# Output products of block 0 ahead of block 1's, its residual and norm among them, and three weight splits in fixed places

## The chip, the cores and the metric

The kernel runs on one core of a Trainium2 chip. The core has five engines with an instruction queue each: TensorE (PE, the matrix products), VectorE (DVE), ScalarE (ACT), GpSimd (POOL) and SyncE (SP, which here issues the weight DMAs). Each engine takes its instructions in order and waits on semaphores for the others. The metric is the device time of one execution in microseconds (us).

## The reference

A two-layer transformer trunk on 256 tokens of width 1024, in f32. Cut to what matters:

```python
def mixer_ab(h, ...):                # layer 0: two groups of attention heads
    ...
    return jnp.concatenate([ya, yb], axis=-1) @ w_out      # 1024 x 1024, "wo"

def squared_relu_mlp(h, w1, w2):
    return jnp.square(jax.nn.relu(h @ w1)) @ w2            # 1024 -> 4096 -> 1024
# every layer, twice (mixer, then MLP):
#   h = x * (1 + scale) + shift                            # "mod", from the conditioning c
#   x = LN(alpha * x + gate * sublayer(h))
```

The scales, shifts and gates ("ada") are products of the conditioning vector with large weights that are read as the kernel runs.

## The kernel before

**Tiles.** The 256 tokens are two blocks, b = 0 and 1, of 128 partitions. Products are done in f32r with both operands split into a high and a low part: `wh`, `wl` for weights, `yTh`, `yTl` for the attention's output transposed, `hTh`, `hTl` for the modulated activations. Each product is three matmuls into one accumulator (`mm3`, L236 to L238). A split is one cast on ACT (L170) and one subtraction on DVE (L171; on POOL for "wo").

**The weight stream.** `plan` is the list of all weight tiles (1 MB each) in the order in which they are used. SP issues their DMAs (L164) into four raw buffers; `take` splits the next tile in two halves into buffers of a pool of six (`wh`) and six (`wl`), so a split waits until earlier products have read the buffer. `need(key)` takes tiles until `key` is there. Tiles of the first MLP are ("w1", 0, i) and ("w2", 0, i); a half is named with a last number, ("w1", 0, 1, 0). The "ada" tiles stand among them.

**Order.** The kernel is written as one program, from which a scheduler makes each engine's order by priority: what was written earlier goes first, among what it expects to be ready. `later(n)` moves what stands in it n places back in priority (negative: ahead); `LATER` is the table of such numbers by step or half tile. A dependency without semaphore (`behind`, used elsewhere in the kernel) only fixes the order of two instructions on one engine.

**The stage around the change.** `mixed_out` runs the output projection of layer 0's mixer. It is driven by strings of steps. The first two run beside the attention of the two blocks ("under"), the third after it:

- Ybj: half j of block b's attention output is transposed (PE, L585), copied and split to yT (ACT L482, L170; DVE L171).
- Obhk: output product of block b, half h of the 1024 columns, half k of the 1024 inputs: 12 matmuls of 128x512 into `ps_out`. O with (h, k) reads weight tile wo_(2h+k). There are two accumulator buffers: (0,0) and (1,0) take them first, then (0,1), (1,1).
- G: the gate row, broadcast.
- Rbh: residual of half h (`residual`): product with the gate (DVE L610, frees the accumulator), plus alpha x (L611), statistics (L612).
- Nb: `norm`: aggregate of the statistics (DVE L616), add epsilon to `rs` (L618), power -1/2 on POOL (L302), then normalise z in two halves (DVE L627).
- Mb: `modulate`: eight PE transposes of z to `ps_mod` (L444), scale and shift to h (ACT L449, for block 1's second half DVE L452), split to hT (L170, L171).

Block 1's M1 and the new x are issued from the MLP: `first_tokens(i, b)` are the first two tiles of the MLP's first product for one block, 24 matmuls of 128x256 into `ps_m` each; `second(i, b, h)` the second product; `first(i)` both blocks at once.

`renew` does R, N, M after the MLP in the same manner, and layer 1's mixer ends in another `mixed_out`, whose strings already have `N0` among block 1's products.

Of the kernel before, what the change touches and what calls it, by code (L numbers as in the profile page):

```python
# [22 lines left out]
ALU = mybir.AluOpType  # L23
# [7 lines left out]
LN_EPS = 1e-5  # L31
# [11 lines left out]
NSPLIT = 6  # L43

SPLITS_LATER, ADA_LATER, ROWS_LATER = 200, 300, 0
LATER = {("ci", 0, 0): -1000, ("ci", 0, 1): -1000, ("co", 1, 1): -300, ("wo", 2, 0): 400, ("ada", 1, 5): 500, "cM1": 30, "cO011": -300, "cO100": 100, "wO000": 60, "wO100": 60, "wO001": 60, "wO010": 60, "wO011": 60, "wO110": -40, "wY10": -80}

X_STEPS = ({8: 4, 9: 4}, 13), ({i: 1 for i in range(3, 11)}, 12)

# [15 lines left out]
def trunk(ctx: ExitStack, tc, c, x, pos, small, ln, ada, w_g, w_g1, w_uq, w_out, c_in, c_out, w1, w2, out):  # L65
    nc = tc.nc
# [19 lines left out]
    def col(shape, name, bufs=4, dtype=F32):  # L86
        return work.tile(shape, dtype, name=name, tag=name, bufs=bufs)


    def by_tensor(key):  # L90

        return key[0] == "ada" and (key[1] == 0 and key[2] >= 8 or key[1] == 1 and key[2] < 6)

    @contextmanager
    def later(n):

        if not n:
            yield
            return
        at = tc.cur_priority  # L100
        tc.cur_priority = at + n
        yield
        tc.cur_priority = at + (tc.cur_priority - at - n)
# [34 lines left out]
    raw, parts, state = {}, {}, {"next": 0, "taken": 0, "half": 0, "critical": None, "rows": None, "copied": None, "columns": None}  # L138
# [5 lines left out]
    def fill():  # L144
        while state["next"] < len(plan) and state["next"] < state["taken"] + NRAW + direct():
            key = plan[state["next"]]
            src = source[key[0]](*key[1:])
            if key[0] in ("g", "g1"):
                cuts, tag = ((0, 712, 1424), "wl") if key[0] == "g" else ((0, 1024), "wh")
                parts[key] = []  # L150
                for lo, hi in zip(cuts, cuts[1:]):
                    t = sp.tile([P, 1024], F32, name="w_" + key[0], tag=tag)[:, :hi - lo]
                    nc.sync.dma_start(t, src[:, lo:hi])
                    parts[key].append(t)
                state["next"] += 1
                if key == ("g1", 0):
                    load_early(1)
                continue
            t = wp.tile([P, 2048], F32, name="w_" + "_".join(map(str, key)), tag="w")
            if key[:2] == ("ada", 0) and key[2] < 8:  # L160
                for j in range(2):
                    nc.sync.dma_start(t[:, j * D:(j + 1) * D], src[:, j * D:(j + 1) * D])
            else:
                nc.sync.dma_start(t[:, :src.shape[1]], src)  # L164
            raw[key] = t
            state["next"] += 1

    def split(dh, dl, src, eng=nc.vector):

        nc.scalar.copy(dh, src)  # L170
        return eng.tensor_sub(dl, src, dh.bitcast(F32))  # L171

    def take():

        key = plan[state["taken"]]
        w = raw.get(key)
        if w is None:
            pass
        elif key[0] == "uq":
            parts[key] = [w[:, :1024], w[:, 1024:]]  # L180
        elif by_tensor(key):
            with later(ROWS_LATER):
                ada_rows(key, w)
        elif key[0] == "ada":
            j = state["half"]
            with later(LATER.get(key, ADA_LATER)):
                state["half"] = ada_product(key, j, w[:, j * D:(j + 1) * D])
            if state["half"]:
                return
        else:  # L190
            cuts = (0, 1024, 2048)
            parts[key] = []
            for part, (lo, hi) in enumerate(zip(cuts, cuts[1:])):
                if key in (("w1", 0, 0), ("w1", 1, 0), ("w2", 0, 15)):
                    wh, wl = (work.tile([P, 1024], F32R, name=n, tag="q4", bufs=5) for n in ("wh", "wl"))
                elif key in (("wo", 0), ("co", 0)):
                    if lo == 0:
                        wide = [t.rearrange("p k q -> p (k q)") for t in new_hT()]
                    wh, wl = wide[0][:, lo:hi], wide[1][:, lo:hi]
                else:  # L200
                    wh = sp.tile([P, 1024], F32R, name="wh", tag="wh")[:, :hi - lo]
                    wl = sp.tile([P, 1024], F32R, name="wl", tag="wl")[:, :hi - lo]
                half = (*key, part)
                with later(LATER.get(half, SPLITS_LATER)):
                    split(wh, wl, w[:, lo:hi], nc.gpsimd if key[0] == "wo" else nc.vector)
                parts[key].append((wh, wl))
        state["taken"] += 1
        fill()
# [10 lines left out]
    def need(key):  # L219
        while place[key] >= state["taken"]:  # L220
            take()
        if by_tensor(key):
            ada_columns()
            ada_end()
        return parts.get(key)
# [75 lines left out]
    def rsqrt(dst, src):  # L301
        state["pow"] = nc.gpsimd.tensor_tensor(out=dst, in0=src, in1=mhalf, op=ALU.pow)  # L302
# [15 lines left out]
    def ada_product(key, j, w):  # L318

        junk = work.tile([P, D], BF16, name="junk", tag="junk", bufs=1)  # L320
        m, bias = ada_bias(key, j)
        state[key, j] = nc.vector.tensor_tensor_reduce(out=junk, in0=w, in1=cB, scale=1.0, scalar=bias,  # L322
                                                       op0=ALU.mult, op1=ALU.add, accum_out=m)
        if j == 1:
            ada_factors(key)
        return 1 - j

    def behind(what, m):

        if what in state:  # L330
            tc.add_manual_dep(m.ins, state[what].ins.name, mybir.DependencyInfo(
                mybir.DependencyClass.NoSync, mybir.DependencyReason.DATA))
# [6 lines left out]
    def ada_rows(key, w):  # L339

        ada_columns()
        ps = pa("ps_ada")
        for k in range(KT):
            g = slice(32 * (k % 4), 32 * (k % 4 + 1))
            in_turn(nc.tensor.matmul(ps[g, :256], cT[:, k:k + 1].to_broadcast([P, 32]),
                                     w[:, 256 * k:256 * (k + 1)], start=k < 4, stop=k >= 4))
        state["rows"] = key, ps
# [85 lines left out]
    def new_hT():  # L435
        return [hp.tile([P, KT, 256], F32R, name=n, tag=n) for n in ("hTh", "hTl")]
# [152 lines left out]
    def new_yT(b):  # L589
        hi = work.tile([P, KT, P], F32R, name="yTh", tag="q4", bufs=5)  # L590
        if b == 0:
            return hi, work.tile([P, KT, P], F32R, name="yTl", tag="q4", bufs=5)
        lo = work.tile([P, 1040], F32R, name="yTl", tag="vv", bufs=2)[:, :D]
        return hi, lo.rearrange("p (n q) -> p n q", n=KT)
# [19 lines left out]
    def moments(st):  # L614
        mv = col([P, 2], "mv")
        nc.vector.bn_aggr(mv, st.rearrange("p a s -> p (a s)"))  # L616
        rs = col([P, 1], "rs")
        nc.vector.tensor_scalar_add(rs, mv[:, 1:2], LN_EPS)  # L618
        rsqrt(rs, rs)
        return mv, rs  # L620

    def norm(b, zst):
        z, st = zst
        mv, rs = moments(st)
        for h in range(2):
            s = slice(h * 512, (h + 1) * 512)
            nc.vector.tensor_scalar(z[:, s], z[:, s], mv[:, 0:1], rs, op0=ALU.subtract, op1=ALU.mult)  # L627

    def new_x(zs, gb):

# [103 lines left out]
    for b in range(NB):  # L734
# [4 lines left out]
                                       op0=ALU.mult, op1=ALU.add, accum_out=ss)  # L739
# [121 lines left out]
    def steps(*todo):  # L861
        for f, *args in todo:
            with later(LATER.get(names[f] + str(args[0]), 0)):
                f(*args)
# [30 lines left out]
    def mixed_out(ys, name, i, first, second, under_first, under_second, after):  # L895
# [7 lines left out]
        def step(s):  # L903
            op, *n = s
            b = int(n[0]) if n else 0
            if op in todo:
                with later(LATER.get(s, 0)):
                    todo[op](b)
            if op == "Y":
                if n[1] == "0":  # L910
                    yT[b] = new_yT(b)
                with later(LATER.get(name[0] + s, 0)):
                    y_half(ys[b], yT[b], int(n[1]))
                if n[1] == "1":
                    zs[b] = new_z()
            elif op == "O":
# [3 lines left out]
                need((name, 2 * h + kq))  # L920
                with later(LATER.get(name[0] + s, 0)):
                    out_part(accs[b, h], yT[b], (name, 2 * h + kq), kq, kq == 0, kq == 1)
# [27 lines left out]
        def rest():  # L950
# [4 lines left out]

    hT, rest = mixed_out(ys, "wo", 0, side(st[4]), side(st[5]),
# [3 lines left out]


    def mlp(l, hT, rest, rows):
# [154 lines left out]
    mv, rs = moments(zs[1][1])  # L1117
    beside_vector(0, slice(672, D), *first, after=state["pow"])
    for s in halves:
        z = zs[1][0]  # L1120
        nc.vector.scalar_tensor_tensor(z[:, s], in0=z[:, s], scalar=mv[:, 0:1], in1=gb[0][:, s],  # L1121
                                       op0=ALU.subtract, op1=ALU.mult)
# [55 lines left out]
```

## Time and profile before

| | us |
|---|---|
| median of 3 runs | 669.85 (668.53 to 671.62) |
| the profiled execution | 669.5 |
| its span in the profile | 667.7 |
| outside the span | 1.8 |
| mean granted PE clock | 0.979 |
| PE busy | 633.5 (95%) |
| DVE busy | 472.7 (71%) |
| ACT busy | 339.8 (51%) |
| POOL busy | 53.6 (8%) |
| DMA, mean over the span | 227 GB/s |

Times in rows of the timeline count from the span's start. The output projection runs until 143, the first MLP from 152 to 341, the MLP's norm and modulation until 351. The name of a tile stands with the line that wrote it: `z<-ps_out,gateB` of L610 is the start of a residual, `wl<-w_w,wh` of L171 a weight split, `z<-z,mv,rs` of L627 a norm. A bracket at a row's end tells how long the engine idled before it and which instruction released it. The granted clock is a share of PE's full clock.

### The profile page before, as it was taken

What the parts mean: (1) busy time and instruction counts of PE and PEld (TensorE: products, weight loads), DVE (VectorE), ACT (ScalarE), POOL (GpSimd) and SP (SyncE); (2) the same over time, 40 slices, a digit from 0 to 9 for tenths busy, and PEclk for the clock granted to TensorE, in tenths of its full rate; (3) what the DMA queues carried; (4) which work ended last, traced back from release to release, by engine and by line L of the source; (5) the groups of instructions that cost most, each with busy time, mean ns of one, the idle gap of its engine ahead of it and who ended that gap; (6) DMA issues with size and microseconds to landing.
All of it is one profiled execution on the core that took longest, in us unless ns stands there. A gap on an engine that the chain in (4) does not pass through costs nothing. (4 is left out here: it accounts for less than half of the span.)

```text
span 667.7 us, 9765 instructions
## 1 busy us (share of the span) xinstructions
PE 633.5 (95%) x3762; PEld 532.3 (80%) x3762; DVE 472.7 (71%) x856; ACT 339.8 (51%) x538; POOL 53.6 (8%) x77
## 2 busy tenths in 40 slices
PE   6998989968999999999989999999999999999994
PEld 3555777857989898988867888888899989898983
DVE  2859998485588889887796996755867755554447
ACT  3324757345554545455544555873654555545440
POOL 5010246100020000100010000000000000000004
PEclk9999998997999999999989999999999999999997
DMA  8993796353588897899843486311467855565101
GB/s 313 407 414 123 264 359 256 126 190 126 189 315 300 322 380 270 330 352 367 311 151 115 171 353 223 140 60 63 151 228 257 310 189 189 200 237 193 66 0 63
DMA packets 24384, 151.50 MB, mean 227 GB/s; under 512 B 2833, under 2 KB 3089, under 8 KB 8338
## 3 DMA queue, kind: packets, MB, share of 16 engines
q1 hardware_dynamic: 24194, 150.71, 61.6%
q8 instruction: 29, 0.48, 0.3%
q10 hardware_dynamic: 144, 0.18, 0.1%
q14 instruction: 17, 0.14, 0.1%
HBM read 149.83 MB, written 1.05 MB: 226 GB/s over the span
## 5 line engine op out<-in xcount | busy, mean ns | idle before, releaser
L171 DVE TENSOR_TENSOR wl<-w_w,wh 128x1024 fp32r<-128x1024 f32 x128 | 153.5, 1221 | 81.3 <-ACT wh L170 81.2
L170 ACT CAST wh<-w_w 128x1024 fp32r<-128x1024 f32 x128 | 131.0, 1050 | 151.6 <-PE ps_m L237 71.0
L236 PE MATMUL ps_m<-hTh,wh 128*128 128x256 f32 x448 | 126.7, 283 | 0.0
L238 PE MATMUL ps_m<-hTh,wl 128*128 128x256 f32 x448 | 126.6, 283 | 0.0
L237 PE MATMUL ps_m<-hTl,wh 128*128 128x256 f32 x448 | 126.6, 283 | 0.0
L322 DVE CUSTOM_DVE_ANT_0 junk<-w_ada,cB,sm 128x1024 bf16<-128x1024 f32 x72 | 95.7, 1328 | 11.1 <-DMA w_ada<-in_ada_dram 9.8
L236 PE MATMUL ps_m<-wh,uh 128*128 128x512 f32 x256 | 101.6, 397 | 0.0
L237 PE MATMUL ps_m<-wl,uh 128*128 128x512 f32 x256 | 101.1, 395 | 0.0
L238 PE MATMUL ps_m<-wh,ul 128*128 128x512 f32 x256 | 101.0, 396 | 0.0
L237 PEld LDWEIGHTS ps_m<-hTl,wh 128*128 128x128 f32 x448 | 85.6, 191 | 1.3
L236 PEld LDWEIGHTS ps_m<-hTh,wh 128*128 128x128 f32 x448 | 85.6, 191 | 1.2
L238 PEld LDWEIGHTS ps_m<-hTh,wl 128*128 128x128 f32 x448 | 85.7, 191 | 0.0
L238 PEld LDWEIGHTS ps_m<-wh,ul 128*128 128x128 f32 x256 | 48.2, 188 | 11.3 <-DVE ul L171 0.2
L236 PEld LDWEIGHTS ps_m<-wh,uh 128*128 128x128 f32 x256 | 48.3, 189 | 10.1 <-ACT uh L170 0.3
L237 PEld LDWEIGHTS ps_m<-wl,uh 128*128 128x128 f32 x256 | 48.2, 188 | 9.7
L236 PE MATMUL ps_c<-wh,hTh 128*128 128x512 f32 x96 | 38.6, 406 | 2.4 <-ACT hTh L170 2.0
L541 ACT ACTIVATE prob<-prob,negm 128x128 f32<-128x128 f32 (+1 forms) x64 | 26.9, 451 | 23.4 <-DVE negm L537 23.4
L171 DVE TENSOR_TENSOR ul<-relu,uh 128x512 fp32r<-128x512 f32 (+1 forms) x36 | 22.7, 630 | 22.7 <-ACT uh L170 22.7
L237 PE MATMUL ps_c<-wl,hTh 128*128 128x512 f32 x96 | 38.8, 405 | 0.0
L238 PE MATMUL ps_c<-wh,hTl 128*128 128x512 f32 x96 | 38.3, 400 | 0.0
L171 DVE TENSOR_TENSOR wl<-w_ci,wh 128x1024 fp32r<-128x1024 f32 x24 | 28.7, 1218 | 5.4 <-ACT wh L170 5.2
L302 POOL TENSOR_TENSOR rs<-rs,mhalf 128x1 f32<-128x1 f32 x8 | 6.6, 824 | 320.5 <-DVE rs L618 320.5
(231 smaller groups left out, 1025.9 us busy)
## 6 DMA issues: line engine op xcount, KB each, us to landing
w_w<-in_w_dram SPq DMA_DIRECT2D x64, 1024.0 KB, 5.1
w_ada<-in_ada_dram SPq DMA_DIRECT2D x40, 1024.0 KB, 6.6
w_ci<-in_c_in_dram SPq DMA_DIRECT2D x12, 1024.0 KB, 5.7
w_ada<-in_ada_dram SPq DMA_DIRECT2D x12, 512.0 KB, 9.5
w_wo<-in_w_out_dram SPq DMA_DIRECT2D x4, 1024.0 KB, 6.1
w_co<-in_c_out_dram SPq DMA_DIRECT2D x4, 1024.0 KB, 5.4
w_g<-in_w_g_dram SPq DMA_DIRECT2D x8, 356.0 KB, 9.1
early<-in_ada_dram SPq DMA_DIRECT2D x4, 512.0 KB, 8.0
```

The costliest lines, as they stand in the source:

```text
L170: nc.scalar.copy(dh, src)
L171: return eng.tensor_sub(dl, src, dh.bitcast(F32))
L236: nc.tensor.matmul(ps, a[0], b[0], start=start, stop=False)
L237: nc.tensor.matmul(ps, a[0], b[1], start=False, stop=False)
L238: nc.tensor.matmul(ps, a[1], b[0], start=False, stop=stop)
L302: state["pow"] = nc.gpsimd.tensor_tensor(out=dst, in0=src, in1=mhalf, op=ALU.pow)
L322: state[key, j] = nc.vector.tensor_tensor_reduce(out=junk, in0=w, in1=cB, scale=1.0, scalar=bias, op0=ALU.mult, op1=ALU.add, accum_out=m)
L541: state["exp"] = nc.scalar.activation(pr[:, j, :nk], pr[:, j, :nk], AF.Exp, bias=negm[:, hd:hd + 1], scale=-1.0)
```

## The change

It does five things:

1. The third string of `mixed_out` begins with O010 and O011, followed by R01, N0 and Y11; O101, O110 and O111 of block 1 follow, with M0 ahead of O101. Before, O010 and O011 stood in the second string, Y11 and O101 came right after R01, and N0 stood with the last product.
2. `BEHIND` ties three half splits on DVE: the first half of w1 tile 1 behind the `rs` of block 0's norm ("moments0"), its second half and the first half of w2 tile 0 behind block 0's norm ("norm0").
3. In `LATER`, steps O001, O010 and O011 lose their 60, O100 goes from 60 to 120 and O101 gets 60.
4. The ada tile (1, 5) loses its 500 and has the usual 300, (1, 6) and (1, 7) get 600.
5. `moments` and `norm` note their instructions for `BEHIND`; this emits nothing.

```diff
-LATER = {... ("wo", 2, 0): 400, ("ada", 1, 5): 500, "cM1": 30, "cO011": -300, "cO100": 100, "wO000": 60, "wO100": 60, "wO001": 60, "wO010": 60, "wO011": 60, "wO110": -40, "wY10": -80}
+LATER = {... ("wo", 2, 0): 400, ("ada", 1, 6): 600, ("ada", 1, 7): 600, "cM1": 30, "cO011": -300, "cO100": 100, "wO000": 60, "wO100": 120, "wO101": 60, "wO110": -40, "wY10": -80}
+
+BEHIND = {("w1", 0, 1, 0): "moments0", ("w1", 0, 1, 1): "norm0", ("w2", 0, 0, 0): "norm0"}
...
                 with later(LATER.get(half, SPLITS_LATER)):
-                    split(wh, wl, w[:, lo:hi], nc.gpsimd if key[0] == "wo" else nc.vector)
+                    behind(BEHIND.get(half), split(wh, wl, w[:, lo:hi], nc.gpsimd if key[0] == "wo" else nc.vector))
...
-        nc.vector.tensor_scalar_add(rs, mv[:, 1:2], LN_EPS)
+        state["moments"] = nc.vector.tensor_scalar_add(rs, mv[:, 1:2], LN_EPS)
...
         mv, rs = moments(st)
+        state["moments%d" % b] = state["moments"]
...
-            nc.vector.tensor_scalar(z[:, s], z[:, s], mv[:, 0:1], rs, op0=ALU.subtract, op1=ALU.mult)
+            state["norm%d" % b] = nc.vector.tensor_scalar(z[:, s], z[:, s], mv[:, 0:1], rs, op0=ALU.subtract, op1=ALU.mult)
...
                          "s1 Y00 | s1 | s1 O000 Y10 | O100",
-                         "G | | Y01 O001 R00 | O010 O011 | R01",
-                         "Y11 O101 | O110 R10 | | O111 N0 | R11 | M0 | N1")
+                         "G | | Y01 O001 R00",
+                         "O010 O011 R01 N0 Y11 | M0 O101 | O110 R10 | O111 R11 | N1")
```

What `behind` does with it:

```python
    def behind(what, m):
        if what in state:
            tc.add_manual_dep(m.ins, state[what].ins.name, ...NoSync...)
```

The order that results is shown at three places. In the names of weight tiles the last number tells them apart: 1037 is w1 tile 0, 1162 w1 tile 1, 1211 w2 tile 0, 1288 w1 tile 2. Lines of the changed kernel are two or three higher.

DVE from the start of R01 (the first multiply) to block 0's norm, before:

```order
L610 TENSOR_TENSOR z<-ps_out,gateB 128x512
L171 TENSOR_TENSOR wl<-w_w_0_0_1037,wh 128x1024
L611 SCALAR_TENSOR_TENSOR z<-x_79,z 128x512
L610 TENSOR_TENSOR z<-ps_out,gateB 128x512
L612 BN_STATS stats<-z 128x6
L611 SCALAR_TENSOR_TENSOR z<-x_81,z 128x512
L616 BN_AGGR mv<-stats 128x2
L171 TENSOR_TENSOR wl<-w_w_0_2_1288,wh 128x1024
L618 TENSOR_SCALAR rs<-mv 128x1
L612 BN_STATS stats<-z 128x6
L627 TENSOR_SCALAR z<-z,mv,rs 128x512 x2
```

And of the changed kernel:

```order
L612 TENSOR_TENSOR z<-ps_out,gateB 128x512
L613 SCALAR_TENSOR_TENSOR z<-x_79,z 128x512
L173 TENSOR_TENSOR wl<-w_w_0_0_1037,wh 128x1024
L614 BN_STATS stats<-z 128x6
L173 TENSOR_TENSOR yTl<-evac,yTh 128x512
L618 BN_AGGR mv<-stats 128x2
L620 TENSOR_SCALAR rs<-mv 128x1
L173 TENSOR_TENSOR wl<-w_w_0_1_1162,wh 128x1024
L630 TENSOR_SCALAR z<-z,mv,rs 128x512 x2
L173 TENSOR_TENSOR wl<-w_w_0_1_1162,wh 128x1024
L173 TENSOR_TENSOR wl<-w_w_0_0_1211,wh 128x1024
```

Block 1's residual (x_81) has left the chain and follows later; the two splits of w1 tile 1, which before came ahead of R01, now stand between rs and the norm and behind the norm.

PE at the end of the output products, before:

```order
L236 MATMUL ps_out<-wh,yTh 128x512
L237 MATMUL ps_out<-wl,yTh 128x512
L238 MATMUL ps_out<-wh,yTl 128x512
L444 MATMUL ps_mod<-ident,z 128x128 x8
L236 MATMUL ps_m_1457<-wh,hTh 128x256
L237 MATMUL ps_m_1457<-wl,hTh 128x256
```

And of the changed kernel, from the tenth product of O111:

```order
L238 MATMUL ps_out<-wh,yTh 128x512
L446 MATMUL ps_mod<-ident,z 128x128 x8
L239 MATMUL ps_out<-wl,yTh 128x512
L240 MATMUL ps_out<-wh,yTl 128x512
L238 MATMUL ps_out<-wh,yTh 128x512
L239 MATMUL ps_out<-wl,yTh 128x512
L240 MATMUL ps_out<-wh,yTl 128x512
L238 MATMUL ps_out<-wh,yTh 128x512
L239 MATMUL ps_out<-wl,yTh 128x512
L240 MATMUL ps_out<-wh,yTl 128x512
L238 MATMUL ps_out<-wh,yTh 128x512
L238 MATMUL ps_m_1457<-wh,hTh 128x256
```

On PE block 1's products now run O110, O111, O101, after block 0's; M0's transposes have moved from behind all products to fourteen large products ahead of their end, and small products of the MLP (`ps_m_1457`) come between the last ones.

DVE at the end of the first MLP, where `renew` begins (x_79 is block 0, x_81 block 1; the w_ci are weights of layer 1), before:

```order
L612 BN_STATS stats<-z 128x6 x2
L171 TENSOR_TENSOR wl<-w_ci_3120,wh 128x1024
L616 BN_AGGR mv<-stats 128x2
L610 TENSOR_TENSOR z<-ps_m_1435,gateB 128x512
L618 TENSOR_SCALAR rs<-mv 128x1
L171 TENSOR_TENSOR wl<-w_ci_3120,wh 128x1024
L627 TENSOR_SCALAR z<-z,mv,rs 128x512 x2
```

And of the changed kernel:

```order
L614 BN_STATS stats<-z 128x6 x2
L612 TENSOR_TENSOR z<-ps_m_1435,gateB 128x512
L618 BN_AGGR mv<-stats 128x2
L173 TENSOR_TENSOR wl<-w_ci_3120,wh 128x1024
L620 TENSOR_SCALAR rs<-mv 128x1
L613 SCALAR_TENSOR_TENSOR z<-x_81,z 128x512
L630 TENSOR_SCALAR z<-z,mv,rs 128x512 x2
```

Block 1's multiply moved ahead of block 0's aggregate, and a split changed places with block 1's add on the way to the norm.

More of the change, by code (lines that the diff above doesn't have):

```diff
@@ L45 @@
 SPLITS_LATER, ADA_LATER, ROWS_LATER = 200, 300, 0
-LATER = {("ci", 0, 0): -1000, ("ci", 0, 1): -1000, ("co", 1, 1): -300, ("wo", 2, 0): 400, ("ada", 1, 5): 500, "cM1": 30, "cO011": -300, "cO100": 100, "wO000": 60, "wO100": 60, "wO001": 60, "wO010": 60, "wO011": 60, "wO110": -40, "wY10": -80}
+LATER = {("ci", 0, 0): -1000, ("ci", 0, 1): -1000, ("co", 1, 1): -300, ("wo", 2, 0): 400, ("ada", 1, 6): 600, ("ada", 1, 7): 600, "cM1": 30, "cO011": -300, "cO100": 100, "wO000": 60, "wO100": 120, "wO101": 60, "wO110": -40, "wY10": -80}
+BEHIND = {("w1", 0, 1, 0): "moments0", ("w1", 0, 1, 1): "norm0", ("w2", 0, 0, 0): "norm0"}
 X_STEPS = ({8: 4, 9: 4}, 13), ({i: 1 for i in range(3, 11)}, 12)
```

## The prediction

> **What bounds the kernel now.** I read the table by stretches first, to find where TensorE (PE) is not full, then PE's list of waits, then PE's timeline at the largest one. The columns of the first view: window and its length, then busy microseconds of PE, PE's weight load, DVE, ACT and POOL, granted clock, DMA share, GB/s.
>
> ```profile
> 140.00:160.00 20.00, 12.72 (x63) 11.17 (x62) 15.24 (x25) 8.89 (x17) 1.24 (x3) 0.74 0.60 209
> 180.00:340.00 160.00, 160.00 (x1005) 143.80 (x1004) 133.51 (x172) 82.69 (x102) 5.88 (x12) 1.00 0.87 322
> 260.00:280.00 20.00, 20.00 (x124) 17.87 (x124) 19.06 (x27) 11.22 (x14) 0.00 (x0) 1.00 0.91 314
> ```
>
> The first MLP, 180 to 340, is 160 of 160 us PE at full clock: there PE's own work is the time, so whatever PE gains ahead of it is kept as long as weights arrive. The hole is 140 to 160: 12.72 busy of 20, and at 0.74 of the clock. PE's list of waits (total, times, longest) names who ends it:
>
> ```profile
> PE ps_mod L444 <- DVE z L627: 6.0, 2, 5.7
> ```
>
> The timeline (start, duration, bracket = idle before and its releaser) gives the place: after the last output product PE waits for the norm of block 0, then for the modulated activations.
>
> ```profile
> 128.59 0.48 PE L236 MATMUL ps_out<-wh,yTh 128*128 128x512 f32 x1
> ...
> 142.88 0.40 PE L238 MATMUL ps_out<-wh,yTl 128*128 128x512 f32 x1
> 148.95 1.94 PE L444 MATMUL ps_mod<-ident,z 128*128 128x128 f32 x8 [5.68 <-DVE z L627]
> 152.49 0.58 PE L236 MATMUL ps_m<-wh,hTh 128*128 128x256 f32 x1 [1.60 <-ACT hTh L170]
> ...
> 157.99 0.30 PE L236 MATMUL ps_m<-wh,hTh 128*128 128x256 f32 x1
> 158.13 0.28 PE L237 MATMUL ps_m<-wl,hTh 128*128 128x256 f32 x1
> ```
>
> Sixty products run from 128.59 to 142.88 at one per 0.23 us (two transposes among them), so the last one's slot ends at 143.11. Twenty-five small products take 152.49 to 157.99, 0.22 each; from 158.13 they take 0.12. Why the norm is so late, DVE shows:
>
> ```profile
> 142.11 0.68 DVE L610 TENSOR_TENSOR z<-ps_out,gateB 128x512 f32<-128x512 f32 x1
> 142.71 1.21 DVE L171 TENSOR_TENSOR wl<-w_w,wh 128x1024 fp32r<-128x1024 f32 x1
> ...
> 145.05 0.68 DVE L612 BATCH_NORM_STATS2 stats<-z 128x6 f32<-128x512 f32 x1
> ...
> 146.36 1.17 DVE L171 TENSOR_TENSOR wl<-w_w,wh 128x1024 fp32r<-128x1024 f32 x1
> 147.45 0.14 DVE L618 TENSOR_SCALAR rs<-mv 128x1 f32<-128x1 f32 x1
> ...
> 148.26 1.00 DVE L627 TENSOR_SCALAR z<-z,mv,rs 128x512 f32<-128x512 f32 x2
> ```
>
> R01, the last half of block 0's residual, is multiplied only at 142.11, and weight splits (wl) and block 1's residual stand between its steps: 6.15 us from multiply to norm, all after PE has run out.
>
> The clock goes with it. The following rows are cut at the edges where the granted clock changes, 3.41 us apart; the column after POOL's is the clock.
>
> ```profile
> 96.59:100.00 3.41, 1.56 (x20) 1.44 (x22) 3.34 (x5) 0.72 (x3) 2.08 (x1) 1.00 1.00 332
> 100.00:103.41 3.41, 3.41 (x25) 2.52 (x15) 1.53 (x12) 3.28 (x6) 1.57 (x1) 0.50 0.88 317
> 140.96:144.37 3.41, 2.32 (x10) 1.52 (x9) 3.40 (x4) 3.00 (x3) 0.13 (x1) 1.00 0.62 187
> 144.37:147.79 3.42, 0.00 (x0) 0.00 (x0) 3.42 (x8) 0.04 (x1) 0.12 (x1) 1.00 1.00 393
> 147.79:151.20 3.41, 1.94 (x8) 1.57 (x8) 2.67 (x6) 1.12 (x4) 0.99 (x2) 0.50 0.38 156
> ```
>
> A window in which PE was busy 1.56 of 3.41 is followed by half clock, as is the empty one; one with 2.32 of 3.41 was not. So a wait costs clock here from somewhere between 1.1 and 1.85 us idle in one window.
>
> **The change, part by part.** Reordering: nothing is added or removed on PE. The order of the program puts O010 and O011 straight after O001, then R01 and N0, with block 1's 36 products after them as cover; M0's transposes enter ten products into O111, and O101 and the first small products follow. What it takes away, if N0 and M0 keep up:
> - the wait for z, from 143.11 to 148.95: 5.84
> - the eight transposes at half clock, 1.94 against 1.05 in layer 1 (below): 0.89
> - the wait for hTh: 1.60
> - 25 small products in 5.50 us instead of 25 x 0.12 = 3.00: 2.50
>
> Together 10.83. Layer 1 already has N0 under block 1's products:
>
> ```profile
> 462.87 0.55 POOL L302 TENSOR_TENSOR rs<-rs,mhalf 128x1 f32<-128x1 f32 x1 [112.76 <-DVE rs L618]
> 463.46 1.00 DVE L627 TENSOR_SCALAR z<-z,mv,rs 128x512 f32<-128x512 f32 x2 [0.73 <-POOL rs L302]
> 464.40 1.05 PE L444 MATMUL ps_mod<-ident,z 128*128 128x128 f32 x8
> 465.31 1.85 ACT L449 ACTIVATE h<-ps_mod,facB,facA 128x128 f32<-128x128 f32 x5
> 467.03 0.63 ACT L170 CAST hTh<-h 128x512 fp32r<-128x512 f32 x1
> ```
>
> Its transposes start with no wait. Does N0 keep up here? Count from the end of O011 (0). DVE, whose half-width operations follow each other every 0.6 us: R01's multiply and add to 1.5, the split of w1 tile 0 to 2.7, statistics to 3.3, yTl to 3.9, aggregate and rs to 4.2. The new dependencies then put the first split of w1 tile 1 between rs and the norm. Its ACT cast needs a buffer that wo_2 holds until half of O110 is done, about 2.4 after O110's wait (below), and ends at 3.5; the split runs 4.2 to 5.4. PE: four transposes 0.5, O110 from 0.9 to 3.7, ten products of O111 to 6.0. The norm's first half must be ready by 6.0.
>
> New waits. (a) O110 needs the accumulator that R01's multiply reads: drain 0.15, multiply 0.68, semaphores about 0.1, less 0.5 of transposes ahead of it: 0.45. All 36 later products stand behind it; bounds 0 (were the transposes longer) and 0.9 (without them).
>
> (b) The split in front of the norm is not free. With DVE idle POOL's power took 0.55, at 462.87 above; beside a split it looks like this:
>
> ```profile
> 477.45 1.46 POOL L302 TENSOR_TENSOR rs<-rs,mhalf 128x1 f32<-128x1 f32 x1 [14.04 <-DVE rs L618]
> 477.29 1.22 DVE L171 TENSOR_TENSOR wl<-w_w,wh 128x1024 fp32r<-128x1024 f32 x1
> 478.95 1.00 DVE L627 TENSOR_SCALAR z<-z,mv,rs 128x512 f32<-128x512 f32 x2 [0.44 <-POOL rs L302]
> ```
>
> The power ends 0.40 after the split's end, the norm starts 0.44 after it. So here the norm starts at 5.4 + 0.44 = 5.85, half of it ends at 6.4, and PE waits 0.4 at the transposes; bounds 0 (a power that is hidden under the split) and 1.9 (the split a further 1.5 late, rival A). The Trainium skill has a rule for this, in "SBUF — State Buffer", section "Who interferes with whom": a DVE instruction with two SBUF inputs holds off a GpSimd instruction that reads SBUF until it is done. The rows agree (1.46 against 0.55); were it otherwise, by a power of 0.55 under the split, the sum would be 0.4 better.
>
> (c) In layer 1 hTh's first half is ready at 467.66, 3.26 after the transposes start. Here PE fills that with the transposes, 1.05, and nine products of 0.23: 3.1, so 0.1 is missing. The second half stands behind one more cast (1.05) on ACT; PE then has 12 small products and the last five large ones. I take 0.1; bounds 0 and 1.05.
>
> (d) Block 1's residual and norm come after O101 and are hidden under block 0's small products and second(0); before, PE waited for its activations twice:
>
> ```profile
> 165.69 0.39 PE L236 MATMUL ps_m<-wh,hTh 128*128 128x256 f32 x1 [0.44 <-ACT hTh L170]
> 167.18 0.39 PE L238 MATMUL ps_m<-wh,hTl 128*128 128x256 f32 x1 [0.76 <-DVE hTl L171]
> ```
>
> That is 1.20; walking DVE's new order I get 1.5, so 0.3 is lost; bounds -1.2 and 1.2.
>
> (e) At the MLP's end DVE's order moves too: block 1's multiply, which waited for PE at 338.56, now stands ahead of the aggregate of block 0, and an add between rs and the norm.
>
> ```profile
> 338.16 0.20 DVE L616 BATCH_NORM_AGGREGATE mv<-stats 128x2 f32<-128x12 f32 x1
> 338.56 0.69 DVE L610 TENSOR_TENSOR z<-ps_m,gateB 128x512 f32<-128x512 f32 x1 [0.20 <-PE ps_m L238]
> 340.88 1.00 DVE L627 TENSOR_SCALAR z<-z,mv,rs 128x512 f32<-128x512 f32 x2 [0.44 <-POOL rs L302]
> ```
>
> The split that ran beside the power now lies ahead of rs, which comes 1.3 later, with an add of 0.6 in its stead beside the power: the norm is about 0.5 later. PE is idle there, so all of it counts; bounds 0 and 0.9.
>
> Weights: the splits move with their buffers; the w1/w2 DMAs on SP wait for those buffers, so they follow the products that free them, up to about 7 us earlier, some (w1 tile 4) only about 4. ada_6 and ada_7 move behind, ada_5 forward: no new work. The MLP's first tiles are split before PE needs them by more than the difference, so 0.
>
> Sum: 10.83 - 0.45 - 0.4 - 0.1 - 0.3 - 0.5 = 9.1. The profiled execution took 669.5 us, span 667.7; the median is 669.85. 669.5 - 9.1 = 660.4 and 669.85 - 9.1 = 660.75: I say 660.5.
>
> **Rivals.** A: the split tied in between rs and norm is late. It stands on PE (O110), ACT's cast and DVE in turn, and norm, transposes and everything behind them wait. What speaks for it: three engines in series with 0.4 us already missing. Against: cover of 22 products. If it is 1.5 late, PE idles 1.9 in one window, which by the 96.59 row brings half clock for 3.4 us, and 3.4 us of products then lose 1.7: 660.5 + 1.5 + 1.7 = 663.7. The Trainium skill's page "TensorE: Matmul & The Clock Gate", section "What's actually happening", lets the clock drop after a window that is idle. By that rule A would cost no clock, 662.0. The 96.59 row, half clock after a window 46% busy, speaks against it.
>
> B: the lead is lost in the MLP, because weights or DVE bound it. For it: DVE 19.06 of 20 at 260 to 280, DMA at 0.87 to 0.91, and
>
> ```profile
> SPq L164 <- DVE wl L171: 328.4, 67, 28.9
> ```
>
> Against it is the same row: the queue waits mostly for DVE to release split buffers, which follow PE; it is not the transfers that are late, and PE is never short from 180 to 340. If half of the 9.1 is lost, 665; all of it, 669.6.
>
> C, slower: block 1's chain, now issued last, arrives after block 0's work is used up. It needs O101, two splits (2.4), three half-width steps, rs, power, norm (1.0), transposes and the scaling: about 8.5 us after O101, while PE has 10 us of block 0's small products and second(0). To be slower it has to come over 9.1 + 1.5 = 10.6 us later than that, or 9 with half clock on the products behind it; 12 would give 660.5 + 10.5 + 1.7 = 672.7. No row shows a delay near that.
>
> **How the numbers follow.** The sum 0.72; A 0.15; B 0.09, of which a third leaves under 3.4 us; C 0.04. Half a per cent, 3.35 us, is about what a measurement of this kernel can tell from no change. Faster 0.89 (the sum, A, most of B), same 0.07 (the rest of B and mild forms of C), slower 0.04. The sum's own range: its upper bounds do not fall together; with (a), (b), (c) and (e) at 0 and (d) at 0 it is 658.7; with (c) and (d) at their worst 662.4. To 8 in 10 I take A in, with room for half of B: 658 to 665.5.
>
> **What would show it.** Right: PE's wait for z L630 under 1 us, transposes near 1.05, 140 to 160 close to 20 busy at clock 1.00, small products every 0.12 us and block 1's first small product some 10 us earlier than at 165.69; POOL's power for block 0 near 1.4. A: a bracket of 1.5 or more before ps_mod and half clock behind it. B: idle PE between 170 and 330. C: a bracket of many us at block 1's first small product. Wrong altogether would be a stall that the order does not show, such as a DMA of w1 tile 1 or 2 that lands late.

## The result, and the profile after

The changed kernel took 660.71 us (median of 4, 659.91 to 661.34) against 669.98 for the kernel before: a ratio of 0.986, 95% interval 0.9834 to 0.9887. In two later comparisons it was 0.9894 (0.9876 to 0.9912) and 0.9894 (0.9877 to 0.9911), so the gain is 7 to 9.3 us. Forecast were 660.5 and a range of 658 to 665.5. Executions of one kernel spread by about 2 us, more than some of the terms below; these are read from traces.

The profiled execution took 661.25 us, its span 659.5, 8.2 less than before. The stretch that had the hole (same columns as in the prediction: after the length come PE, weight load, DVE, ACT, POOL, granted clock, DMA share and GB/s):

```profile
140.00:160.00 20.00, 18.68 (x125) 16.07 (x125) 18.21 (x31) 12.02 (x26) 0.69 (x2) 1.00 0.50 174
```

PE is busy 18.68 of 20 us at full clock, before 12.72 at 0.74. PE's timeline from 134 to 157, all rows with a wait and the first small products:

```profile
134.64 0.50 PE L238 MATMUL ps_out<-wh,yTh 128*128 128x512 f32 x1 [0.35 <-DVE z L612]
...
140.28 1.08 PE L446 MATMUL ps_mod<-ident,z 128*128 128x128 f32 x8 [0.23 <-DVE z L630]
...
143.36 0.38 PE L238 MATMUL ps_m<-wh,hTh 128*128 128x256 f32 x1
143.58 0.28 PE L239 MATMUL ps_m<-wl,hTh 128*128 128x256 f32 x1
...
153.24 1.08 PE L446 MATMUL ps_mod<-ident,z 128*128 128x128 f32 x8 [0.23 <-DVE z L630]
156.11 0.39 PE L238 MATMUL ps_m<-wh,hTh 128*128 128x256 f32 x1 [0.85 <-ACT hTh L172]
```

Block 0's transposes start at 140.28 where it was 148.95, take 1.08 and wait 0.23; the first small product stands under no wait. And the chain that releases them, on DVE and POOL:

```profile
133.90 0.69 DVE L612 TENSOR_TENSOR z<-ps_out,gateB 128x512 f32<-128x512 f32 x1 [4.99 <-PE ps_out L240]
...
137.80 0.15 DVE L620 TENSOR_SCALAR rs<-mv 128x1 f32<-128x1 f32 x1
137.91 1.23 DVE L173 TENSOR_TENSOR wl<-w_w,wh 128x1024 fp32r<-128x1024 f32 x1
139.59 1.00 DVE L630 TENSOR_SCALAR z<-z,mv,rs 128x512 f32<-128x512 f32 x2 [0.45 <-POOL rs L304]
138.03 1.52 POOL L304 TENSOR_TENSOR rs<-rs,mhalf 128x1 f32<-128x1 f32 x1 [16.65 <-DVE rs L620]
```

From R01's multiply to the norm it is 5.69 us, before 6.15: the chain is hardly shorter. It now begins 8.2 us sooner (133.90, before 142.11) and lies under block 1's products.

How far PE is ahead of the kernel before, at the same product in both traces. About 0.6 us of the lead is there before the changed stage begins; the section on the prediction comes back to it.

| place | before | after | lead |
|---|---|---|---|
| first product of second(0) | 161.20 | 150.77 | 10.43 |
| first product of second(0) for block 1 | 172.95 | 162.81 | 10.14 |
| second products near the MLP's end | 334.18 | 324.27 | 9.91 |
| transposes after the MLP | 341.57 | 332.34 | 9.23 |
| projection of layer 1, wait for rope | 356.36 | 347.33 | 9.03 |
| its transposes of q | 391.84 | 383.64 | 8.20 |
| last second products of layer 1 | 656.95 | 648.73 | 8.22 |

### The profile page after: what moved, and what is told of

Read it like the earlier page. It is cut to its first block, busy times and chain, and to the rows that moved or that the text cites. A ratio compares the mean times of both kernels' runs of the same rounds, so it can differ in the third digit from the quotient of the medians.

```text
span 659.5 us, 9766 instructions
## 1 busy us (share of the span) xinstructions
PE 629.7 (95%) x3762; PEld 528.4 (80%) x3762; DVE 472.4 (72%) x856; ACT 338.7 (51%) x538; POOL 57.3 (9%) x77
```

## The experiments

The theory: the gain is idle time of PE that block 1's products now cover, and the clock that this idle time had cost; it needs the order on PE that comes out of the scheduler. The rivals: the written order alone, the tied splits or the ada tiles carry it; or the clock has no share. Four kernels ran together, with the kernel before at 668.87 us.

**Without the ties.**

```diff
-BEHIND = {("w1", 0, 1, 0): "moments0", ("w1", 0, 1, 1): "norm0", ("w2", 0, 0, 0): "norm0"}
+BEHIND = {}
```

> The changed kernel without the three ties (BEHIND empty); strings and LATER as changed. Theory (the gain is the cover of block 0's norm and modulation by block 1's products, which the order on PE gives): on DVE a split of 1.2 us comes ahead of rs and another beside the power, so the norm is about 1.2 us later, and on PE the eight transposes stand 4 products (0.93 us) further back; PE waits under 1 us more, the clock stays at 1.00 between 140 and 160, 660.5 to 662. Rival (the ties carry the gain, since without them the splits fall into the norm's chain): the wait for z comes back with 2 us or more and half clock behind it, 664 or more.

Measured: 660.84 us, ratio 0.9873 (0.9856 to 0.989). PE's rows with a wait:

```profile
140.14 1.08 PE L446 MATMUL ps_mod<-ident,z 128*128 128x128 f32 x8 [0.28 <-DVE z L630]
144.58 0.39 PE L240 MATMUL ps_m<-wh,hTl 128*128 128x256 f32 x1 [0.39 <-DVE hTl L173]
```

The norm is later here, and the scheduler has set the transposes four products further back, so the wait is 0.28. The ties don't carry the gain.

**The new strings alone**, with the old LATER and no ties.

> The kernel before with the changed step strings alone; LATER as before and no ties. Theory: what counts is the order on PE that comes out, not the order in which the steps are written; here all 60 output products still stand ahead of block 0's transposes on PE and splits and block 1's residual stand in the norm's chain on DVE, so the wait for z (4 to 6 us), the half clock and the wait for hTh stay: 668 to 670.5. Rival (the written order carries the gain): 661 to 664.

Measured: 668.66 us, ratio 0.9996 (0.9984 to 1.0007): nothing.

```profile
148.16 1.94 PE L446 MATMUL ps_mod<-ident,z 128*128 128x128 f32 x8 [5.25 <-DVE z L630]
151.70 0.58 PE L238 MATMUL ps_m<-wh,hTh 128*128 128x256 f32 x1 [1.60 <-ACT hTh L172]
```

The old wait stands where it stood. The strings set the order in which steps are written; with the old numbers in LATER the scheduler mixes block 0's last products with block 1's again.

**The old strings** with the new LATER and the ties.

> The changed kernel with the old step strings; LATER and the ties as changed. On PE block 0's products now run under block 1's attention and 24 of block 1's products come behind the first 12 small products. Theory: cover between O011 and the transposes is only 12 products and block 1's last attention steps, about 4 us for a chain of about 5, and nothing stands between transposes and the first small product, so PE waits 1 to 2 us for z and about 2 us for hTh, with half clock for one or two stretches of 3.4 us: 664 to 667. Rival (LATER alone carries the gain): 660 to 662.

Measured: 665.21 us, ratio 0.9941 (0.9928 to 0.9955), about half of the gain.

```profile
138.30 0.63 PE L446 MATMUL ps_mod<-ident,z 128*128 128x128 f32 x4 [0.59 <-DVE z L630]
139.82 0.66 PE L446 MATMUL ps_mod<-ident,z 128*128 128x128 f32 x4 [0.68 <-ACT evac L484]
142.09 0.58 PE L238 MATMUL ps_m<-wh,hTh 128*128 128x256 f32 x1 [1.61 <-ACT hTh L172]
...
140.00:160.00 20.00, 17.74 (x94) 15.07 (x94) 12.19 (x20) 10.68 (x21) 1.60 (x2) 0.83 0.35 112
```

z is waited for 0.59 us, not the 1 to 2 expected. In its place PE waits 0.68 for ACT to copy block 1's yT, whose transposes stand between the two halves of block 0's, and 1.61 for hTh, and the clock falls (0.83 over the stretch).

**The old wait, filled.** The kernel before with products whose result nobody reads, 24 behind the last output product and 6 behind the transposes.

```diff
+            elif op in ("J", "K"):
+                n = {"J": 24, "K": 6}[op]
+                junk = pc("ps_junk")
+                for k in range(n):
+                    nc.tensor.matmul(junk, yT[1][0][:, k % 8], yT[1][0][:, 4:8]..., start=k == 0, stop=k == n - 1)
...
-                         "Y11 O101 | O110 R10 | | O111 N0 | R11 | M0 | N1")
+                         "Y11 O101 | O110 R10 | | O111 J N0 | R11 | M0 K | N1")
```

> The kernel before with 24 more products of 128x512 behind the last output product and 6 more behind block 0's transposes; they read block 1's yT and nothing reads their result. The waits for z and hTh stay where they are, but PE is busy in them. Theory (about 3.4 of the 9 us gained are clock, the rest is idle time): granted clock 1.00 from 147.8 to 158, transposes in 1.05 to 1.1 us, small products every 0.12 us, the first second product about 3 us earlier, 666 to 667.5. Rival (the clock's share is nothing, or it falls for another reason than PE's idling): 669 to 671.5.

Measured: 666.65 us, ratio 0.9961 (0.9947 to 0.9975).

```profile
141.99 5.64 PE L933 MATMUL ps_junk<-yTh 128*128 128x512 f32 x24
...
147.83 1.09 PE L444 MATMUL ps_mod<-ident,z 128*128 128x128 f32 x8 [0.20 <-DVE z L627]
150.05 1.66 PE L933 MATMUL ps_junk<-yTh 128*128 128x512 f32 x6 [1.14 <-ACT h L449]
151.56 0.28 PE L236 MATMUL ps_m<-wh,hTh 128*128 128x256 f32 x1
151.67 0.28 PE L237 MATMUL ps_m<-wl,hTh 128*128 128x256 f32 x1
...
140.00:160.00 20.00, 18.66 (x112) 15.70 (x111) 14.56 (x25) 9.30 (x19) 1.24 (x3) 1.00 0.56 206
```

With no useful work moved, PE kept busy is at clock 1.00, its transposes take 1.09 instead of 1.94 and the small products 0.12 instead of 0.22. That is worth 0.39%, 2.6 us (1.7 to 3.5). From the last output product to second(0) it is 18.32 us before and 16.01 here, 2.3 less; the six products behind the transposes came late, since they waited 1.14 for a buffer, and held the small products up a little. So about a third of the gain of 7 to 9.3 us is clock, and what is left is the idle time itself.

Three more kernels ran together with the changed kernel (before: 668.95), and another three with the changed kernel again (before: 669.19).

> The changed kernel itself, to compare the next three on one chip. Theory and rivals alike: 0.986 of the kernel before (0.984 to 0.988); power of block 0's norm 1.4 to 1.55 us, wait at the transposes 0.2 to 0.4, wait for block 1's hTh 0.8.

Measured: 661.91 us, 0.9894 (0.9876 to 0.9912). The ratio lies outside the 0.984 to 0.988 that was expected, though the interval reaches into it: the gain is 7.1 us here, 2 less than in the first comparison. Power 1.51, waits 0.23 and 0.85, as expected.

> The changed kernel once more, to compare the next three on one chip: 0.986 to 0.990 of the kernel before, as in its two comparisons so far.

Measured: 661.77 us, 0.9894 (0.9877 to 0.9911).

**The split behind the norm** instead of ahead of it.

```diff
-BEHIND = {("w1", 0, 1, 0): "moments0", ...
+BEHIND = {("w1", 0, 1, 0): "norm0", ...
```

> The changed kernel with the first split of w1 tile 1 tied behind block 0's norm, where it was tied behind rs. Theory (the split beside POOL's power delays it): the power takes 0.55 us again and the norm starts about 0.85 us earlier after rs; on PE the transposes stand 4 products further ahead, so the wait there stays at 0.2 to 0.5, and the total is within 1 us of the changed kernel. Rival (the power is long for another reason than the split): the power stays at 1.4 or more and PE waits 0.9 or more at the transposes.

Measured: 660.77 us, ratio 0.9883 (0.9865 to 0.9901), no different from the changed kernel's 0.9894.

```profile
138.54 0.56 POOL L304 TENSOR_TENSOR rs<-rs,mhalf 128x1 f32<-128x1 f32 x1 [16.94 <-DVE rs L620]
...
139.83 1.08 PE L446 MATMUL ps_mod<-ident,z 128*128 128x128 f32 x8 [0.20 <-DVE z L630]
...
156.49 0.39 PE L238 MATMUL ps_m<-wh,hTh 128*128 128x256 f32 x1 [1.09 <-ACT hTh L172]
```

The power is 0.56 us with the split away from it and 1.51 with it: the split delays POOL. The scheduler set the transposes four products further ahead, as it expected the norm sooner, so PE's wait is 0.20 as against 0.23.

**The norm after the MLP.** Here the 0.97 us that PE waits (row below) was to be taken away.

```diff
+BEHIND = {..., ("ci", 1, 0): "norm0"}
...
-        nc.vector.scalar_tensor_tensor(z[:, s], in0=xt[b][:, s], ...)
+        m = nc.vector.scalar_tensor_tensor(z[:, s], in0=xt[b][:, s], ...)
+        if b:
+            behind("norm0", m)
```

> The changed kernel with two more ties: the first split of weight tile 1 of layer 1's projection and block 1's add stand behind block 0's norm, which matters where the norm is taken after the first MLP. Theory (that norm lies on PE's path, and a split ahead of rs and an add beside the power delay it): power 0.55 us, norm 1.2 to 1.5 us earlier against the end of the MLP's products, PE's wait before those transposes 0 to 0.3 in place of 0.97, total 0.7 to 1.3 us below the changed kernel. Rival (block 1's later add or the later split is then waited for, or the weights' arrival in the projection bounds it): within 0.3 us of the changed kernel.

Measured: 662.13 us, ratio 0.9897 (0.9879 to 0.9914). The rival holds. The changed kernel's two waits there are the first two rows, from its first trace; the next three are this kernel's:

```profile
332.34 1.08 PE L446 MATMUL ps_mod<-ident,z 128*128 128x128 f32 x8 [0.97 <-DVE z L630]
347.33 0.47 PE L238 MATMUL ps_c<-wh,hTh 128*128 128x512 f32 x1 [0.83 <-DVE rope L476]
```

```profile
331.01 0.55 POOL L304 TENSOR_TENSOR rs<-rs,mhalf 128x1 f32<-128x1 f32 x1 [54.27 <-DVE rs L622]
332.29 1.08 PE L446 MATMUL ps_mod<-ident,z 128*128 128x128 f32 x8
349.11 0.47 PE L238 MATMUL ps_c<-wh,hTh 128*128 128x512 f32 x1 [2.64 <-DVE rope L476]
```

The wait for the norm is gone and the power is 0.55, but the wait for rope grew from 0.83 to 2.64. DVE has no idle time between the two blocks' norms except for the power, so what block 0's norm gained was waited for behind block 1's. The longer wait costs clock as well: from 350 to 353 the granted clock is 0.50 here and 1.00 in the changed kernel's first trace.

**Both edits.**

> Both of the two edits before on the changed kernel. Theory: the effects add, 0.7 to 1.8 us below the changed kernel. Rival: nothing is gained over the changed kernel, within 0.3 us.

Measured: 662.65 us, ratio 0.991 (0.9894 to 0.9927): nothing gained, as the rival had it. The wait for rope is 2.64 here too.

**Strings and the numbers of the output steps only**: no ties, and the ada tiles as before.

```diff
-LATER = {... ("ada", 1, 6): 600, ("ada", 1, 7): 600, ...
+LATER = {... ("ada", 1, 5): 500, ...
-BEHIND = {("w1", 0, 1, 0): "moments0", ...
+BEHIND = {}
```

> The kernel before with the new step strings and only the numbers of the wo steps from the new LATER; no ties, ada tiles as before. Theory (strings and the numbers of the output products together set PE's order, and that order is the gain): within 1 us of the changed kernel, PE's waits from 133 to 150 together under 1.5 us, clock 1.00 there. Rival (the ada tiles' new places or the ties carry part of it): 2 us or more slower than the changed kernel.

Measured: 660.9 us, ratio 0.9884 (0.9865 to 0.9903), the changed kernel's gain. With the strings alone at 0.9996 this shows that strings and the numbers of the output steps carry it together, and neither the ties nor the ada tiles are needed. What the numbers of the output steps give alone was not run: the kernel with the old strings had the ties and the new ada numbers besides.

**The scaling after the MLP on ACT**, to relieve DVE where the experiment on that norm had shown it full.

```diff
-                if h == 0 or b == 0:
+                if h == 0 or b == 0 or i == 2:
                     nc.scalar.activation(t[:, j], ...)
                 else:
                     nc.vector.tensor_scalar(t[:, j], ...)
```

> The changed kernel with the scaling of block 1's second half after the MLP done on ACT in place of DVE (four operations of 0.4 us). Theory (behind the MLP DVE is full between the two norms, and PE waits for its rope steps): the rope steps come up to 1.1 us earlier, PE's wait of 0.8 for rope shrinks to 0 to 0.2, total 0.4 to 0.9 us below the changed kernel. Rival (the late hTl of block 1, now behind eight operations on ACT, is waited for instead): within 0.3 us or slower.

Measured: 660.21 us, ratio 0.9879 (0.986 to 0.9898). PE no longer waits for rope at that place. The median is 1.6 us below the changed kernel, more than the 0.4 to 0.9 expected, but the intervals overlap.

**The same without ties.**

> The changed kernel without the three ties and with the scaling on ACT as before. Theory (the ties are worth nothing, since without them block 1's transposes and activations are not waited for, which pays for the later norm): 0.5 to 2 us below the changed kernel. Rival: the ties are worth about 1 us, total at the changed kernel's time or above.

Measured: 659.91 us, ratio 0.9867 (0.9848 to 0.9886), the lowest median of the study, 1.9 below the changed kernel beside it; here too the intervals overlap. What the ties cost is plainer in the traces. From the first product of O110 to the first product of layer 1's projection the changed kernel takes 200.78, 200.79 and 200.75 us in its three traces, and the three kernels without ties 200.17, 200.18 and 200.16. The ties cost 0.6 us there. Without them PE waits 0.28 for block 0's z and 0.39 for its hTl, and no wait shows for block 1; with them it waits 0.23, and then 0.23 and 0.85 for block 1, which is 0.64 more.

## Why the prediction was right

What it said of the mechanism holds at the places that it named: the wait for the norm and the half clock behind it are gone, the new waits at O110 and at the transposes came in the sizes given, and the norm after the MLP got later. That the first median, 660.71, lies 0.2 us from the forecast is in part luck. The two later comparisons give 7.1 us (5.9 to 8.3), less than the sum of 9.1; inside the stated range are all three medians.

The prediction counts a wait from the end of the last product's slot (0.23 us for a large product), a bracket from the end of its row, which lies about 0.16 us later. The terms are compared here as the prediction counted them.

- **Removed, 10.83.** When 36 output products are left and y's transposes are done, PE is at 134.74 in the trace of before (142.88 less 35 slots) and at 134.14 here. From there to second(0) it is 26.46 us before and 16.63 here, 9.83 less; forecast were 10.83 - 0.45 - 0.4 - 0.1 = 9.88. The filled wait shows that the clock's part, forecast at 0.89 and 2.50, is real: 2.6 us (1.7 to 3.5) in the whole.
- **(a)** O110's wait was put at 0.45 and is 0.50 (bracket 0.35). PE's last product ends at 133.86, the multiply starts 0.04 later, and O110 0.05 after the multiply's end: these two gaps are what the term called semaphores, 0.1.
- **(b)** The wait at the transposes was put at 0.4 and is 0.40 (139.88 to 140.28, bracket 0.23); the power takes 1.52 and ends 0.41 after the split, as the row of layer 1 had it (1.46, 0.40). The Trainium skill's rule on this, "SBUF — State Buffer", section "Who interferes with whom", agrees with the 0.56 that came when the split was moved away. Yet taking the split away from the power did not take the wait away: the scheduler then set the transposes four products further ahead, and the bracket stayed at 0.20.
- **(c)** hTh's first half was put 0.1 late and is 0.07 late (143.29 to 143.36).
- **(d)** For block 1, 0.3 was to be lost: 1.5 by the walk through DVE's order against 1.20 before. But the 1.20 is of brackets. Counted by slots the waits are 1.53 before and 1.57 here, so next to nothing is lost in them. The lead shrinks by 0.3 all the same between the first and second row of the table: about half of that is a product of a later tile that stands ahead of the second place here (0.16 at 162.65). Where the rest lies, and another 0.2 in the MLP, I did not settle. That the number fits is luck.
- **(e)** The norm after the MLP was to cost 0.5 and costs 0.68 (a wait of 0.97, before 0.29).

The table's lead of 10.43 is 0.6 more than the 9.83 of the stage. It was there at 134.14 already. At the first output product the changed kernel is still 0.29 behind (104.99, before 104.70); what differs between these places is mainly the clock (same columns), before and after:

```profile
113.60:117.00 3.40, 3.40 (x14) 2.93 (x13) 3.40 (x11) 1.95 (x4) 0.00 (x0) 0.51 0.96 333
```

```profile
113.60:117.00 3.40, 2.75 (x19) 2.10 (x18) 3.40 (x11) 1.75 (x5) 0.00 (x0) 1.00 0.79 299
```

Behind a wait of 1.60 us for the tile bcrows the clock is 0.51 in the trace of before; behind one of 1.65 for the same tile it is 1.00 in this one. In the ten traces with the new strings and the new numbers of the output steps the clock falls there in four, in the four others in all. So this loss comes and goes among kernels with the same steps there, and whether the change has a part in the 0.6 stays open. Without it the lead at the end, 8.2, would be 7.6, near the 7.1 of the later comparisons.

Not in the sum was the way behind the MLP. The wait for rope in layer 1's projection went from 0.40 to 0.83, and in the first trace a weight tile was late there. ACT's cast of it, after and before:

```profile
378.05 2.01 ACT L172 CAST wh<-w_ci 128x1024 fp32r<-128x1024 f32 x2 [2.27 <-DMA w_ci<-in_c_in_dram]
```

```profile
386.27 2.00 ACT L170 CAST wh<-w_ci 128x1024 fp32r<-128x1024 f32 x2 [1.50 <-DMA w_ci<-in_c_in_dram]
```

These are 8.2 apart, with PE 9.0 ahead until then: 0.8 us of the lead went into one transfer, and q's transposes behind it waited 0.71. PE's waits for q are 2.1 us in all in this trace, 1.4 and 1.8 in the changed kernel's other two, and 1.4 in the trace of before: this loss differs from execution to execution. Rival B had looked for such a loss inside the MLP, where the table shows 0.2; this one came after it and was a tenth of the gain.

Rival A did not come, since the split was in time and the scheduler keeps the transposes near the norm. The price that it put on idle time was right in kind: with the old strings 2.9 us of waits, none over 1.61, brought the stretch to 0.83 of the clock. Rival C's chain was waited for 1.08, not many microseconds.

## What to carry to other kernels

A chain on the vector engines that takes almost as long as before (5.69 us for 6.15) costs little once enough independent products run beside it on the tensor engine (0.40 us of wait for 5.84); look first at what the order puts there, and only then at shortening the chain. Where a scheduler makes the order, the written order and the priorities act together: look at the order that comes out, since half of such an edit may do nothing (0.9996 here) and fixed dependencies may cost more than they bring (0.6 us for the three). Before taking a wait away, see whether the engine that ends it is full behind it, for then the wait only moves (0.97 gone, 0.83 became 2.64).

## What was not expected of the hardware

POOL's power on 128x1 took 0.55 to 0.56 us with DVE idle, as much beside a statistics step of 0.68 (at 147.67 in the trace of before), 0.86 beside a DVE add of 0.68 and 1.51 beside a split of 1.22, and in both the latter it ended about 0.41 after the DVE instruction. So its length tells what DVE did beside it rather than anything of the power itself.

The same waits don't always cost clock. Behind the MLP all three traces of the changed kernel show waits of 0.97 and 2.00 us; in two of them the granted clock is 0.50 for about 3.4 us behind these, in the third it stays at 1.00.
